# Order edges on VectorE in the transition from cross-attention to the FFN of a hybrid decoder layer

## The chip, the cores and the metric

The kernel runs on one core of a Trainium2 chip. The metric is the device time of one execution in microseconds (us). The median of three runs of the kernel before is 1662.94 us (1659.94 to 1664.27).

## What is computed

One decoder layer over 1024 rows of width 1024, in float32: a sparse and a differential attention with one input projection, a cross-attention to 256 memory rows, and a gated FFN with a causal convolution of width 3. The change touches the seam between the last two:

```python
h = h + cross_attention(rmsnorm(h, g_xattn), rmsnorm(mem, g_mem), w_xq, w_xk, w_xv, w_xo, g_xq, g_xk)
h = h + conv_glu(rmsnorm(h, g_ffn), w_ffn_in, conv_w, conv_b, w_ffn_out)

def rmsnorm(x, g):
    return x * rsqrt(mean(x * x, axis=-1) + EPS) * g

def conv_glu(hn, w_ffn_in, conv_w, conv_b, w_ffn_out):
    a, gate = split(hn @ w_ffn_in, 2)                 # 1024 x 2816 each
    conv = conv_b + sum(a_pad[:, j:j + S] * conv_w[j] for j in range(3))
    return (gelu(conv) * gate) @ w_ffn_out
```

## The kernel before, in words

**Arithmetic.** Every float32 product is made of three matmuls on high and low parts (mm3, lines 307 to 310). So each operand is split first: ScalarE or GpSimd casts the high part, VectorE or GpSimd subtracts it for the low part (L201, L203 and L204 for weights, L1330 and L1333 for activations). The FFN's input product is a block scheme with seven products instead of eight (P1, P2, P3, T1, T2, T3, T4 below), on sums and differences of quarter blocks. The activations' blocks are B11, B21, B22 and the sums T1 to T4; the weights' sums are made anew for each f.

**Rows and weights.** The 1024 rows are eight row blocks t of 128 rows. The FFN's 2816 columns are 22 groups f of 128. The weights of one f come as two raw tiles (a and g) and go through five jobs in this order: A (two pages from a), S (three VectorE additions, L225 to L227: `ws`, g and a change in place), B (two pages and one more subtraction, L233), C (two pages), D (one page). A page is a high and a low part, ready for TensorE; there are 12 page buffers. There are two raw buffers in the transition and a third from f = 1 on, and the next load (L188, on SyncE's queue, which issues nothing else there) starts when the last reader of a raw buffer is done. `W.pump(n)` (line 260) traces up to n jobs if pages are free by its own count; `W.get` traces jobs until the wanted page exists.

**The transition (lines 1603 to 1615).** For t = 0 to 7: `xo_unit(1, t)` (line 1287) makes the second half of the cross-attention's output product of row block t, adds it into h2[t] on VectorE (L1298), and in the middle of its matmuls calls `f_tr(t - 2)`; it ends with `W.pump(1)`. Then `f_norm(t)` (line 1303) normalizes: the squares are summed on ScalarE (L1133), `rstd1` (line 129) makes the reciprocal root with two VectorE instructions (L133, L134: the second is the first guess) and ten dependent ScalarE instructions on one column (L137), and two VectorE instructions scale the row block (L1313). `f_tr(t)` (line 1365) transposes the row block on TensorE (L1379). For t below 4 it splits the halves into B11 and B21. For t from 4 on it makes block sums: VectorE adds high and low part of B11 (L1344), GpSimd those of B21 (L1344), VectorE the low part of B22 (L1333), a piece of T1 (L1392) and of T2 (L1394), GpSimd pieces of T3 and T4 (L1396, L1398). Both PSUM buffers named trp are in use while one row block is transposed.

**After the loop** follow: P1 of f = 0 (on B11), `f_tr(6)`, P2 (on B21) with its addition (L1453), `f_tr(7)`, P3 (on B22, with a page of job C), the split of T1 to T3 (1024 columns each, L1358 and L1359) and T4, and then T2, T1, T3, T4 of f = 0. For f from 1 to 21 `ffn_in` (line 1447) makes seven products, seven VectorE additions that empty PSUM (L1453), a convolution (ScalarE L1494, VectorE L1495 and L1496), a gelu (L1497) and a product on GpSimd (L1502). GpSimd also makes sums for the FFN's output product (L1549). The second raw pool and the work tiles of f = 1 take over the memory of the transition's work tiles.

**What sets the order.** Each engine runs its instructions in a fixed order that is made when the kernel is built. The builder walks a simulated timeline and, for each engine, takes the first ready instruction in the order of tracing. Inside `manual_schedule` TensorE's own instructions keep the order of tracing among themselves. For the other engines nothing but readiness and that order decides, so later work that is ready passes earlier work that waits.

By trace order in the kernel before, the jobs of f = 0 are traced here: A in `xo_unit(1, 0)`, S in `xo_unit(1, 1)`, B in `xo_unit(1, 2)`, C in `xo_unit(1, 7)`, D with T2.

Of the kernel before, what the change touches and what calls it, by code (L numbers as in the profile page):

```python
# [11 lines left out]
BF = mybir.dt.bfloat16  # L12
I32 = mybir.dt.int32
AF = mybir.ActivationFunctionType
OP = mybir.AluOpType
# [5 lines left out]
D = 1024  # L21
NT = 8
# [22 lines left out]
def hybrid_layer(ctx, tc, I, out):  # L45
    nc = tc.nc
    pe, act, dve, pool, sp = nc.tensor, nc.scalar, nc.vector, nc.gpsimd, nc.sync
# [81 lines left out]
    def rstd1(r, ss, scale):  # L129

        w = small("rst", (P, 3, 8), 4)
        m, y, t, u = (w[:, 0, j:j + 1] for j in range(4))
        dve.tensor_scalar(m, ss, scale, EPS, op0=OP.mult, op1=OP.add)  # L133
        dve.tensor_scalar(y.bitcast(I32), m.bitcast(I32), -0.5, 1597463007.0, op0=OP.mult, op1=OP.add)  # L134

        def mul(o, x, f, bias=0.0):
            act.activation(o, x, AF.Copy, bias=bias, scale=f)  # L137
        mul(t, y, y)
        mul(t, t, m)
        mul(t, t, -3.0 / 16, 9.0 / 16)  # L140
        mul(y, y, t)
        mul(t, y, y)
        mul(t, t, m)
        mul(u, t, 64.0 / 9, -10.0 / 3)
        mul(t, t, u)
        mul(t, t, 64.0 / 9, 5.0)
        mul(r, t, y)


    NRAW, NWP = 2, 12  # L150
# [125 lines left out]
    W = Weights()  # L276
# [673 lines left out]
    for s in range(-4, NB):  # L950
        h, i = b_units[max(s, 0)]
        m = s % NT
# [178 lines left out]
    def norm_rows(src, jk, ssq, r):  # L1131

        act.activation(jk, src, AF.Square, accum_out=ssq)  # L1133
        rstd1(r, ssq, 1.0 / D)

    hx, hx_h = {}, {}

# [146 lines left out]
    h2 = []  # L1284
    hf, hst = {}, {}

    def xo_unit(c, t, mid=None):
        pages = W.get(("xo", c), 8)
        half, u = divmod(t, 4)
        p = accp()  # L1290
        for k in range(KT):
            oh, ol = ox[k // 4, (k % 4) // 2, half]
            s = slice(u * P, (u + 1) * P)
            if k == 4 and mid:
                mid()
            mm3(p, oh[:, k % 2, s], ol[:, k % 2, s], pages[k][:, 0, :], pages[k][:, 1, :], k == 0, k == KT - 1)
        hs = h2[t][:, c * 512:(c + 1) * 512]
        dve.tensor_tensor(hs, p, hs, op=OP.add)  # L1298
        if t == NT - 1:
            W.free(8)  # L1300
        W.pump(1)

    def f_norm(t):
        rs = slice(t * P, (t + 1) * P)
        act.dma_start(h2_d[rs, :], h2[t])
        st = small("st", (P, 12), 6)
        ws = [w2([P, 512], F32, "hn") for _ in range(1 if t >= 4 else 2)]
        norm_rows(h2[t], ws[0].bitcast(BF), st[:, 0:1], st[:, 1:2])
        hn = []
        for g in range(2):  # L1310
            hg = h2[t][:, g * 512:(g + 1) * 512]
            w = hg if t >= 4 else ws[g]
            dve.scalar_tensor_tensor(w, hg, st[:, 1:2], gff[g], op0=OP.mult, op1=OP.mult)  # L1313
            hn.append(w)
        hst[t] = hn

# [46 lines left out]
    def f_tr(t):  # L1365
        half, u = divmod(t, 4)
        if t == 0:
            xb_new("B11")
            xb_new("B21")
        if t == 4:  # L1370
            xb_new("B22")
            for n in ("T1", "T2", "T3"):
                tf[n] = [page([P, 2, 512], F32, n) for _ in range(2)]
        hn = hst.pop(t)
        ps_ = []
        for g in range(2):
            p = trp()
            for j in range(4):
                pe.transpose(p[:, j * P:(j + 1) * P], hn[g][:, j * P:(j + 1) * P], ident)  # L1379
            ps_.append(p)  # L1380
            if half == 0:
                xb_put(("B11", "B21")[g], u, p, "a", "d")
        if half == 0:
            return
        x11, x21 = xb_sum("B11", u, dve), xb_sum("B21", u, pool)
        ss = slice(u * P, (u + 1) * P)
        t1, t2, t3 = ([tf[n][v][:, :, ss] for v in range(2)] for n in ("T1", "T2", "T3"))
        t4s.append(x21)
        vs = [slice(0, 256), slice(256, 512)]
        xb_put("B22", u, ps_[1], "a", "d")  # L1390
        for v in range(2):
            dve.tensor_tensor(t1[v], two(ps_[0][:, vs[v]]), two(x11[:, vs[v]]), op=OP.subtract)  # L1392
        for v in range(2):
            dve.tensor_tensor(t2[v], two(ps_[1][:, vs[v]]), t1[v], op=OP.subtract)  # L1394
        for v in range(2):
            pool.tensor_tensor(t3[v], t2[v], two(x11[:, vs[v]]), op=OP.subtract)  # L1396
        for v in range(2):
            pool.tensor_tensor(two(x21[:, vs[v]]), two(x21[:, vs[v]]), t2[v], op=OP.subtract)  # L1398
# [28 lines left out]
    gff = []  # L1427
# [3 lines left out]
    for t in range(4, NT):  # L1431
        xo_unit(0, t)
# [169 lines left out]

    with tc.manual_schedule(engines={mybir.EngineType.PE}):
        for t in range(NT):
            xo_unit(1, t, (lambda: f_tr(t - 2)) if t >= 2 else None)
            f_norm(t)
        first = ffn_in(0)
        next(first)
        f_tr(6)
        next(first)  # L1610
        f_tr(7)
        next(first)
        for n in ("T1", "T2", "T3", "T4"):
            xb_finish(n)
        for _ in first:
            pass
# [119 lines left out]
```

## Time and profile before

| | us |
|---|---|
| median of three runs | 1662.94 |
| the profiled execution, whole | 1662.24 |
| its span, first to last instruction | 1660.4 |
| TensorE busy in the span | 1572.2 (95%) |
| VectorE busy | 1208.5 (73%) |
| ScalarE busy | 803.7 (48%) |
| GpSimd busy | 639.1 (38%) |
| mean granted TensorE clock | 0.978 |

The transition lies near 940 to 1045 us of the span, the FFN's input products run on to about 1447 us, the output products to the end. Times in the rows are counted from the span's start. A share of busy time is a mean over all stages of the kernel.

### The profile page before, as it was taken

The page shows a single profiled execution, that of the slowest core. Times are in us where ns is not written, and L with a number is a line of the kernel's source. Part 1 is how long each engine was busy: PE and PEld are TensorE (multiplying, and loading weights), DVE is VectorE, ACT ScalarE, POOL GpSimd, SP SyncE. Part 2 cuts the span into 40 slices and gives each one's busy share as a digit, 9 for nine tenths or more (in the row PEclk, how much of TensorE's full clock was granted, in tenths as well). Part 3 has the DMA queues.
Part 4 walks back from the last instruction along what each step waited for, and adds up shares of the span by engine and source line. Part 5 has one row for each costly group of instructions (what it writes and reads, how often), then busy time and mean ns, then how long its engine had stood idle before and what let it go on. Part 6 is the DMA issues. An engine that isn't in the chain of part 4 may idle for free.

```text
span 1660.4 us, 22257 instructions
## 1 busy us (share of the span) xinstructions
PE 1572.2 (95%) x7596; PEld 1271.6 (77%) x7596; DVE 1208.5 (73%) x2356; ACT 803.7 (48%) x1696; POOL 639.1 (38%) x888
## 2 busy tenths in 40 slices
PE   8899898888789999999999997999999999999999
PEld 7788675666668888878777775888887777888887
DVE  5738888878868875345544379989999999855554
ACT  6556665677877446428442265433333333343432
POOL 2735776223351131031101023666666666551111
PEclk9999998989989999999999998999999999999999
DMA  8320236221210122152203121455555555799812
GB/s 284 102 83 32 91 128 216 77 78 47 64 64 27 52 96 70 67 181 102 89 1 114 40 97 57 167 191 179 176 180 180 183 184 179 262 361 366 305 52 76
DMA packets 112162, 220.06 MB, mean 133 GB/s; under 512 B 18480, under 2 KB 38448, under 8 KB 112048
## 3 DMA queue, kind: packets, MB, share of 16 engines
q1 hardware_dynamic: 91072, 148.37, 26.7%
q0 software_dynamic: 18384, 61.36, 10.4%
q10 hardware_dynamic: 2592, 8.91, 1.4%
q8 instruction: 60, 0.98, 0.2%
q14 instruction: 54, 0.44, 0.1%
HBM read 160.92 MB, written 57.67 MB: 132 GB/s over the span
## 4 chain that ended last, share of the span: by engine, by line
PE 68%; DVE 16%; DMA 6%; ACT 4%; issue 3%; POOL 2%; SPq 0%; ACTq 0%; POOLq 0%; DVEq 0%
PE acc L308 11%; PE acc L310 10%; PE acc L309 10%; PE big L309 4%; PE big L308 4%; PE big L310 4%; PE trp L308 3%; PE trp L309 3%; PE trp L310 3%; PE acc L1036 3%; PE acc L885 2%; DVE jk L565 2%; DVE wp L204 2%; PE trp L691 2%; PE big L1275 2%
## 5 line engine op out<-in xcount | busy, mean ns | idle before, releaser
L204 DVE TENSOR_TENSOR wp<-raw,wp 128x512 fp32r<-128x512 f32 (+1 forms) x184 | 186.1, 1021 | 28.1 <-ACT wp L201 17.8
L201 ACT CAST wp<-raw 128x512 fp32r<-128x512 f32 (+1 forms) x184 | 108.3, 614 | 178.0 <-DVE raw L227 121.0
L1600 DVE TENSOR_TENSOR wp<-fo,wp 128x1024 fp32r<-128x1024 f32 x77 | 102.4, 1344 | 76.8 <-ACT wp L1599 69.2
L1549 POOL TENSOR_TENSOR fs<-fs,fs 128x512 f32<-128x512 f32 x88 | 128.5, 1460 | 64.3 <-DMA fs<-u_d 49.1
L1599 ACT CAST wp<-fo 128x1024 fp32r<-128x1024 f32 x77 | 79.8, 1049 | 107.9 <-PE trp L310 43.1
L308 PE MATMUL acc<-wp,xh 128*128 128x512 f32 (+1 forms) x272 | 109.6, 405 | 3.0 <-ACT X L646 3.0
L309 PE MATMUL acc<-wp,xh 128*128 128x512 f32 (+1 forms) x272 | 109.0, 401 | 0.0
L310 PE MATMUL acc<-wp,xl 128*128 128x512 f32 (+1 forms) x272 | 108.7, 400 | 0.0
L553 ACT ACTIVATE mb<-sc,cand 128x384 bf16<-128x384 f32 (+1 forms) x96 | 75.4, 786 | 35.9 <-DVE cand L557 30.5
L203 POOL TENSOR_SCALAR wp<-raw 128x512 fp32r<-128x512 f32 (+1 forms) x36 | 24.5, 685 | 176.8 <-DVE rst L110 63.6
L682 ACT COPY pt<-trp 128x512 f32<-128x512 f32 (+3 forms) x144 | 66.1, 475 | 40.6 <-PE trp L691 40.3
L1036 PEld LDWEIGHTS acc<-va_t,pt 128*128 128x128 f32 x576 | 75.2, 196 | 9.1 <-ACT pt L682 7.2
L1036 PE MATMUL acc<-va_t,pt 128*128 128x65 f32 x576 | 77.8, 274 | 3.7 <-ACT pt L682 3.6
L1646 POOL TENSOR_TENSOR hr<-hr,r 128x512 f32<-128x512 f32 x16 | 26.8, 1691 | 114.6 <-DVE r L1662 62.9
L1018 DVE CUSTOM_DVE_ANT_0 ea<-big,mb,ra 128x384 f32<-128x384 f32 (+5 forms) x48 | 45.4, 945 | 28.7 <-PE trp L691 25.1
L308 PEld LDWEIGHTS acc<-wp,xh 128*128 128x128 f32 x272 | 52.4, 193 | 15.0 <-ACT X L646 3.7
L1497 ACT ACTIVATE fc<-fc 128x1024 f32<-128x1024 f32 x22 | 23.4, 1062 | 82.9 <-DVE fc L1496 82.8
L204 POOL TENSOR_TENSOR wp<-raw,wp 128x512 fp32r<-128x512 f32 x36 | 47.2, 1325 | 40.5 <-ACT wp L201 40.1
L1019 ACT ACTIVATE ea<-ea,sta 128x128 f32<-128x128 f32 (+7 forms) x64 | 49.6, 776 | 25.7 <-DVE sta L1018 23.5
L1494 ACT ACTIVATE fc<-fa,cw 128x1024 f32<-128x1024 f32 x22 | 27.4, 1244 | 71.4 <-DVE fa L1453 71.4
L309 PEld LDWEIGHTS acc<-wp,xh 128*128 128x128 f32 x272 | 52.3, 192 | 11.3 <-issue 0.2
L310 PEld LDWEIGHTS acc<-wp,xl 128*128 128x128 f32 x272 | 52.1, 192 | 11.4
(422 smaller groups left out, 5113.7 us busy)
## 6 DMA issues: line engine op xcount, KB each, us to landing
raw<-in_w_ffn_in_dram SPq DMA_DIRECT2D x44, 512.0 KB, 4.1
fs<-in_w_ffn_out_dram POOLq DMA_DIRECT2D x44, 256.0 KB, 3.5
ws_d<-fs POOLq DMA_DIRECT2D x44, 256.0 KB, 2.3
fs<-u_d POOLq DMA_DIRECT2D x44, 256.0 KB, 3.8
us_d<-fs POOLq DMA_DIRECT2D x44, 256.0 KB, 3.2
fo<-us_d SPq DMA_DIRECT2D x44, 256.0 KB, 5.4
fo<-ws_d SPq DMA_DIRECT2D x44, 256.0 KB, 5.4
u_d<-fg POOLq DMA_DIRECT2D x21, 512.0 KB, 3.7
```

The lines of the kernel that those rows point to most:

```text
L201: act.copy(pg[:, 0, :n], src)
L204: (dve if el == "d" else pool).tensor_tensor(pg[:, 1, :n], src, pg[:, 0, :n].bitcast(F32), op=OP.subtract)
L308: pe.matmul(o, lhsT=lh, rhs=rh, start=start, stop=False)
L309: pe.matmul(o, lhsT=lh, rhs=rl, start=False, stop=False)
L310: pe.matmul(o, lhsT=ll, rhs=rh, start=False, stop=stop)
L553: act.activation(mb[i], sc[i], AF.Sign, bias=cf[:, j:j + 1], scale=-1.0, accum_out=cnt[:, j:j + 1])
L682: act.copy(dst, src)
L1019: last["act"] = act.activation(e[:, :n], e[:, :n], AF.Exp, bias=st[:, 0, h:h + 1], scale=-1.0)
L1036: pe.matmul(acc[:, hh * 65:hh * 65 + 65], lhsT=pt, rhs=va_t[:, kt, :], start=kt == 0, stop=kt == i)
L1549: pool.tensor_tensor(o, p, q, op=op)
L1599: act.copy(hi, raw)
L1600: dve.tensor_tensor(lo, raw, hi.bitcast(F32), op=OP.subtract)
```

## The change

`rstd1` and `norm_rows` return the VectorE instruction of the first guess (L134), and `f_norm` returns that one and its last scaling instruction (L1313): `guess` and `scaled`. `tc.issue_after(x)` lets every VectorE instruction traced inside its block be ordered behind x on VectorE. It is an order only, not a wait for x to finish, and it binds no other engine.

- The unit `xo_unit(1, 7)`, with `f_tr(5)` in it, comes behind the guess of row block 6.
- `f_tr(6)` comes behind the guess of row block 7.
- P2's addition, and the first weights' jobs S and B, come behind the scaling of row block 7. P1 carries no VectorE instruction.
- In the second pass (c = 1) `xo_unit` doesn't pump while the next job is an S. So after A of f = 0 nothing is pumped; S and B of f = 0 are traced by a new `W.pump(2)` between `f_tr(6)` and P2, and C by P3's `W.get`.

No instruction is added or taken away.

```diff
-        dve.tensor_scalar(y.bitcast(I32), m.bitcast(I32), -0.5, 1597463007.0, op0=OP.mult, op1=OP.add)
+        guess = dve.tensor_scalar(y.bitcast(I32), m.bitcast(I32), -0.5, 1597463007.0, op0=OP.mult, op1=OP.add)
...
+        return guess
...
-        rstd1(r, ssq, 1.0 / D)
+        return rstd1(r, ssq, 1.0 / D)
...
         if t == NT - 1:
             W.free(8)
-        W.pump(1)
+        if c == 0 or W.jobs[W.nsplit][4] != "S":
+            W.pump(1)
...
-        norm_rows(h2[t], ws[0].bitcast(BF), st[:, 0:1], st[:, 1:2])
+        guess = norm_rows(h2[t], ws[0].bitcast(BF), st[:, 0:1], st[:, 1:2])
...
-            dve.scalar_tensor_tensor(w, hg, st[:, 1:2], gff[g], op0=OP.mult, op1=OP.mult)
+            scaled = dve.scalar_tensor_tensor(w, hg, st[:, 1:2], gff[g], op0=OP.mult, op1=OP.mult)
...
+        return guess.ins, scaled.ins
...
         for t in range(NT):
-            xo_unit(1, t, (lambda: f_tr(t - 2)) if t >= 2 else None)
-            f_norm(t)
+            with tc.issue_after(guess) if t == NT - 1 else ExitStack():
+                xo_unit(1, t, (lambda: f_tr(t - 2)) if t >= 2 else None)
+            guess, scaled = f_norm(t)
         first = ffn_in(0)
-        next(first)
-        f_tr(6)
-        next(first)
+        with tc.issue_after(scaled):
+            next(first)
+        with tc.issue_after(guess):
+            f_tr(6)
+        with tc.issue_after(scaled):
+            W.pump(2)
+            next(first)
         f_tr(7)
         next(first)
```

## Rows read from the trace of the kernel before

**Rows 1.** The page: busy tenths in 40 slices, then one line of DMA issues.

```profile
PE   8899898888789999999999997999999999999999
DVE  5738888878868875345544379989999999855554
...
raw<-in_w_ffn_in_dram SPq DMA_DIRECT2D x44, 512.0 KB, 4.1
```

**Rows 2.** Windows: length, busy us (count) PE, PEld, DVE, ACT, POOL; PEclk; DMA, GB/s.

```profile
940.00:950.00 10.00, 10.00 (x46) 8.20 (x45) 7.92 (x12) 2.58 (x5) 0.14 (x1) 1.00 0.32 105
...
995.00:1000.00 5.00, 0.00 (x0) 0.00 (x0) 5.00 (x9) 3.37 (x10) 5.00 (x6) 0.89 0.60 207
1000.00:1005.00 5.00, 1.27 (x6) 1.30 (x7) 5.00 (x7) 2.58 (x14) 2.42 (x3) 0.50 0.00 0
...
1035.00:1040.00 5.00, 5.00 (x23) 3.98 (x22) 4.25 (x6) 1.79 (x3) 0.00 (x0) 1.00 0.82 276
1040.00:1045.00 5.00, 5.00 (x23) 4.03 (x22) 3.13 (x6) 3.17 (x4) 3.88 (x4) 1.00 0.54 176
...
1280.00:1300.00 20.00, 18.57 (x79) 14.34 (x79) 18.86 (x20) 6.50 (x10) 14.34 (x16) 1.00 0.59 197
```

**Rows 3.** Timeline of TensorE in the transition: start, length, line; in brackets idle before.

```profile
1003.73 1.94 PE L1379 MATMUL trp<-ident,h 128*128 128x128 f32 x8 [9.10 <-issue]
...
1022.52 0.50 PE L309 MATMUL big<-T,wp 128*128 128x512 f32 x1 [1.16 <-DVE T L1359]
```

**Rows 4.** Timeline of VectorE, 988 to 1006 us.

```profile
988.21 1.21 DVE L204 TENSOR_TENSOR wp<-raw,wp 128x512 fp32r<-128x512 f32 x1
...
993.04 0.14 DVE L134 TENSOR_SCALAR rst<-rst 128x1 int32<-128x1 int32 x1
...
995.86 2.59 DVE L1344 TENSOR_TENSOR xf<-B,B 128x256 f32<-128x256 f32 x3
998.37 1.21 DVE L225 TENSOR_TENSOR ws<-raw 128x512 f32<-128x512 f32 x1
999.50 0.14 DVE L134 TENSOR_SCALAR rst<-rst 128x1 int32<-128x1 int32 x1
...
1002.89 1.40 DVE L1313 SCALAR_TENSOR_TENSOR h<-h,st,gff 128x512 f32<-128x512 f32 x2
...
1004.82 1.40 DVE L1313 SCALAR_TENSOR_TENSOR h<-h,st,gff 128x512 f32<-128x512 f32 x2
```

**Rows 5.** Timeline of ScalarE: the column chain of row block 0.

```profile
951.27 2.63 ACT L137 ACTIVATE rst<-rst 128x1 f32<-128x1 f32 x9 [0.41 <-DVE rst L134]
...
954.14 0.29 ACT L137 ACTIVATE st<-rst 128x1 f32<-128x1 f32 x1 [0.24 <-ACT rst L137]
```

**Rows 6.** Timeline of VectorE: first and last instruction of S and B, f = 0.

```profile
945.10 0.69 DVE L225 TENSOR_TENSOR ws<-raw 128x512 f32<-128x512 f32 x1 [0.22 <-DMA raw<-in_w_ffn_in_dram]
...
949.21 0.68 DVE L204 TENSOR_TENSOR wp<-ws,wp 128x512 fp32r<-128x512 f32 x1
```

**Rows 7.** Timeline of VectorE: first convolution step of f = 2 and of f = 19.

```profile
1070.17 1.46 DVE L1495 SCALAR_TENSOR_TENSOR fc<-fa,cw,fc 128x1023 f32<-128x1023 f32 x1 [0.78 <-ACT fc L1494]
...
1418.04 1.46 DVE L1495 SCALAR_TENSOR_TENSOR fc<-fa,cw,fc 128x1023 f32<-128x1023 f32 x1 [0.78 <-ACT fc L1494]
```

**Rows 8.** Timeline of TensorE: T4 of f = 2, of f = 3, last idle time.

```profile
1064.73 0.39 PE L308 MATMUL big<-T,wp 128*128 128x512 f32 x1
...
1084.33 0.39 PE L308 MATMUL acc<-T,wp 128*128 128x512 f32 x1
...
1410.47 0.50 PE L308 MATMUL acc<-T,wp 128*128 128x512 f32 x1 [0.94 <-DVE fa L1453]
```

**Rows 9.** Waits of TensorE, 1024 us to the end: total, times, longest.

```profile
PE acc L308 <- DVE fa L1453: 2.4, 2, 1.4
PE big L308 <- DVE fa L1453: 1.0, 2, 0.6
PE trp L308 <- DVE fa L1453: 1.0, 1, 1.0
```

## The prediction

> **What bounds the kernel now.** I read the page's slices first [rows 1]. TensorE is at nine tenths nearly everywhere; slice 25 of 40, 996 to 1038 us, falls to seven tenths: the transition. VectorE is at eight or nine tenths from there to slice 35. So at the seam two engines are candidates, and the change moves work from one place on VectorE to another.
>
> The windows show how the seam fails [rows 2]. From 995 to 1000 us TensorE does nothing and VectorE has no free moment. TensorE's timeline gives the size: 9.10 us idle ahead of the transposes of row block 6, and 1.16 us ahead of T2 [rows 3]. The granted clock is 0.89 from 995 to 1000 us and 0.50, the lower level of 1.2 GHz, from 1000 to 1005 us [rows 2]; the stretch before it is the idle one. VectorE's timeline says why [rows 4]: the guess of row block 6 starts at 993.04, its scaling only at 1002.89. ScalarE needs 951.27 to 954.43, 3.2 us, for the column chain between them when nothing disturbs it [rows 5]. In between VectorE makes block sums (three L1344, 2.59 us) and the first sum of the weights of f = 1 (L225, 1.21 us) ahead of row block 7's guess at 999.50, and ScalarE's fixed order mixes the two chains. That is what the edges forbid.
>
> Next, whether this lost time reaches the end. TensorE passes T4 of f = 2 at 1064.73 and T4 of f = 3 at 1084.33: 19.60 us for one f [rows 8]. VectorE's first convolution step starts at 1070.17 for f = 2 and at 1418.04 for f = 19: 347.87 us for 17 steps, 20.46 us each [rows 7]. So VectorE is slower by 0.86 us per f, 14.6 us over the 17. TensorE waited only 2.4 + 1.0 + 1.0 = 4.4 us in all that time, always for the VectorE additions that empty PSUM [rows 9], last at 1410.47 [rows 8]. The other 10 us went into lead: TensorE ran further and further ahead until PSUM was full. My reading: from the transition to 1410 us VectorE sets the pace, and TensorE has some 10 us to give away. A microsecond that TensorE wins at the seam is waited out later; one that VectorE loses there arrives at the end.
>
> **The change, part by part.**
>
> *The edges on the guesses.* They take L204 (1.21 us), L1344 and others from between the scaling of row block 5 and the guess of row block 6 [rows 4]. That scaling ends where L204 starts, at 988.21, and the squares are ready by then, so the guess falls from 993.04 to about 988.6. With the chain (3.2 us, and about 0.5 for casts in between) the scaling of row block 6 can start near 992.5. Row block 7 depends on the last output product, which doesn't move; I put its guess at 995.2 (before 999.50), its chain's end at 998.9, and `scaled` done at about 1000.4 (before 1004.82 + 1.40 = 1006.2). So the transposes of row block 6 start near 995 instead of 1003.73, and most of the 9.10 us goes.
>
> *What is late next.* S, B and C of f = 0 now all stand behind `scaled`, and P3 needs a page of C. From 1000.4 VectorE has S (3), B (3), C (2) and P2's addition, nine instructions at 0.68 us [rows 6], 6.1 us, and among them the pieces of `f_tr(7)`, some 2 us. So P3 starts near 1008 to 1009. In the kernel before it followed the 1003.73 transposes, P2 and `f_tr(7)`, which I put at 1012.5 by their lengths at the low clock. TensorE is then some 4 us earlier, no longer 9: a second idle stretch takes the place of the first. Behind these instructions on VectorE queue T1 to T3; TensorE's T2 waits for them.
>
> *S and B moved.* Before, they ran from 945.10 to 949.89, with one output addition of 0.6 us between, so 4.2 us [rows 6], where VectorE had 2.1 us of 10 free [rows 2] and no one waited. Now they lie in a stretch where VectorE has no idle time until 1035. The cover is gone: +4.2 us on VectorE. Bounds: 6 x 0.68 = 4.1, and 6 x 1.21 = 7.3 if all meet GpSimd as L225 and L204 did in the seam [rows 4].
>
> *What runs beside GpSimd.* The same instruction has 0.68 us when GpSimd is idle [rows 6] and 1.21 us beside its block sums [rows 4]. The jobs A and S of f = 1 now come after the block sums; S, B, C of f = 0 take their place. Bounds: none, and nine instructions cheaper by 0.53, -4.8 us. I take -1.5, near none, because one set replaces another.
>
> *New idle time on VectorE.* Two chains of 3.2 us, 6.3 us in all, in which VectorE may not run ahead. It is still allowed the pieces of row block 5, the output addition and one scaling under the first, and the pieces of row block 6 under the second, about as much. Bounds 0 and 3; I take 1.
>
> *The idle time of before.* VectorE was idle 0.75 us in 1035 to 1040 and 1.87 us in 1040 to 1045 [rows 2], where work of f = 1 waited for the memory and the end of f = 0. f = 0 now ends earlier, but the weights of f = 1 come later: the load of its first raw tile waits for the last page of C, and has 4.1 us to landing [rows 1]. SyncE's queue has nothing else behind it; VectorE's own queue does, if a sum of f = 1 stands ahead. Bounds 0 and -2.6; I take -1.2.
>
> The casts of S, B and C on ScalarE and GpSimd's block sums carry no edge; they follow their inputs, and they are no new work. Nothing else is added.
>
> *Sum for VectorE.* 4.2 - 1.5 + 1.0 - 1.2 = +2.5 us at the point where the loop over f has its steady order, and with that order, which comes from buffers and pages and not from the seam, +2.5 us at the end. The profiled execution took 1662.24 us, 0.70 below the median. 1662.24 + 2.5 = 1664.7 us. The ends of the terms give 4.1 - 4.8 + 0 - 2.6 = -3.3 and 7.3 + 0 + 3 + 0 = +10.3.
>
> A rule bears on the choice of engine. In 1280 to 1300 us weight loads fill 14.34 of 20 us and VectorE 18.86 [rows 2]. The Trainium skill (Perfetto Trace Analysis, Identifying the Most-Contended Engine) judges TensorE by its weight loads and not by matmul busy time, and improves the engine with the highest occupancy; by that rule VectorE is the engine here, and the trace agrees. The same page (Optimization Strategies) says to treat whatever blocks an idle matmul engine, since its idle time is the loss; that is the rival below.
>
> **The rivals.**
>
> *Faster: TensorE sets the pace.* If VectorE's 20.46 us per f are only a shadow of late inputs and its order behind the seam gets looser, TensorE's gain at P3 stays: 4 us, with the 1.16 us before T2 5 us: 1662.24 - 5 = 1657 us; with the whole 9.10 us, 1653. For it speaks that TensorE is busy over nine tenths and VectorE has about a tenth of idle time in the loop. Against it: all 4.4 us of TensorE's waits are for VectorE, and TensorE's lead grew by 10 us without any wait of VectorE for TensorE in the rows I read. Perfetto Trace Analysis (Optimization Strategies) of the Trainium skill would give this side; the rows bear it out at the seam and not behind it.
>
> *Slower: the first weights come too late.* S, B and C are a chain across VectorE and ScalarE, and the raw buffers of f = 0 come free only after C and D; so the weights of f = 1 start some 8 to 10 us later than before. The place is the stretch from P3 to f = 1's T2. If VectorE has to stand idle there for the loads, by more than the 2.6 us that it stood idle before, or if S and B meet GpSimd at 1.21 us, its delay is 7.3 - 1.5 + 1 + 0 = +6.8 and more: 1669 us. The point from which it decides is 5 us of VectorE delay at the convolution of f = 2.
>
> *The edges do nothing.* If the builder's order already had the guesses first, only the move of S and B would be left, +4 us. The rows speak against it: L1344 and L225 stand right ahead of row block 7's guess [rows 4]. It lies inside the forecast's band.
>
> **How the numbers follow.** Within 0.3% is 5.0 us of 1662.94, about what a measurement of this kernel can tell from no change: 1657.9 to 1667.9. Forecast 1664.7, no measurable change: 0.50. TensorE's gain stays, faster: 0.26. The late weights, slower: 0.24. Both sides leave a tail out of the range: 1656 below (the first rival's 1657 with 1 us for the spread of runs) and 1670.5 above (the second's 1669 and 1.5). The likeliest case's own range is 1659 to 1668.
>
> **What would show it.** Right: the guess of row block 6 starts near 989 and that of row block 7 near 995; the 9.10 us gap ahead of the transposes of row block 6 is under 2 us; a new idle stretch of 5 us or more stands ahead of P3; TensorE's T4 of f = 2 is earlier by some 4 us while L1495 of f = 2 is later by 0 to 5 us and the step per f stays near 20.46; TensorE's waits for L1453 after 1024 us grow from 4.4 to 10 us or more. Wrong: the step per f changes, which would make the pace of VectorE no constant of the loop; or L1495 of f = 2 comes earlier than 1070.17 by more than 3 us, which would mean that my sum for VectorE misses a saving; or TensorE's waits don't grow though it starts earlier.

## The result, and the profile after

The changed kernel takes 1679.95 us (median of 4 runs, 1674.93 to 1684.11) beside 1661.76 us for the kernel before on the same chip: 1.0106 times as long, with a 95% interval of 1.0082 to 1.0130, some 18 us. The profiled execution of the changed kernel took 1684.11 us with a span of 1682.3. That is the slowest of its four runs, so the delays read from its trace add up to more than 18 us. Its output addition of row block 2 starts 0.64 us later than before (960.10 against 959.46); "net" below means that such an offset is taken off. This point lies behind the old place of S and B: ahead of it, at the last output addition of the first half, the offset is 1.23 us (942.70 against 941.47). So the kernels that hold S and B back win 0.6 us there, and their net delays, counted from row block 2, are 0.6 us larger than counted from ahead of the change.

VectorE's timeline in the transition (start, length, engine, line; in brackets the idle time before), to be read against [rows 4]. Line numbers are higher by up to 3 in the changed kernel, and in some experiments by more: L134 is the guess, L1315 the scaling, L226 the first of S, L205 a low part, L1347 a block sum.

```profile
989.00 0.15 DVE L134 TENSOR_SCALAR rst<-rst 128x1 int32<-128x1 int32 x1
...
996.15 0.15 DVE L134 TENSOR_SCALAR rst<-rst 128x1 int32<-128x1 int32 x1
996.22 3.33 DVE L1347 TENSOR_TENSOR xf<-B,B 128x256 f32<-128x256 f32 x4
...
1001.99 2.23 DVE L1315 SCALAR_TENSOR_TENSOR h<-h,st,gff 128x512 f32<-128x512 f32 x2
1004.15 1.21 DVE L226 TENSOR_TENSOR ws<-raw 128x512 f32<-128x512 f32 x1
...
1014.10 2.94 DVE L205 TENSOR_TENSOR wp<-raw,wp 128x512 fp32r<-128x512 f32 x3
```

Both guesses come earlier, by 4.0 and 3.4 us, as the edges want. The last scaling ends at 1004.2 and not at 1000.4. From there to the last low part of C, at 1017.0, it is 12.9 us, where I had counted 6.1 and 2.

TensorE's timeline, to be read against [rows 3]:

```profile
996.19 0.63 PE L1382 MATMUL trp<-ident,h 128*128 128x128 f32 x4 [0.52 <-DVE rst L133]
...
1003.19 1.09 PE L1382 MATMUL trp<-ident,h 128*128 128x128 f32 x4 [3.56 <-issue]
...
1010.71 0.79 PE L309 MATMUL big<-B,wp 128*128 128x512 f32 x1 [5.26 <-ACT wp L202]
...
1016.49 0.79 PE L311 MATMUL big<-B,wp 128*128 128x512 f32 x1 [4.56 <-DVE wp L205]
```

The stall of 9.10 us ahead of row block 6 is 0.52 us now, inside its transposes. In its place stand 3.56 us ahead of row block 7, 5.26 us ahead of P3 and 4.56 us inside it, for the high and the low parts of f = 0's weights: with the 0.52 they are 13.9 us. The windows (columns as in [rows 2]) show what follows for the clock:

```profile
1000.00:1005.00 5.00, 1.72 (x7) 1.38 (x8) 4.56 (x8) 1.06 (x4) 3.32 (x5) 0.72 0.00 0
1005.00:1010.00 5.00, 0.45 (x3) 0.05 (x1) 5.00 (x10) 4.05 (x7) 0.94 (x1) 0.50 0.00 0
...
1015.00:1020.00 5.00, 3.51 (x8) 2.81 (x9) 5.00 (x6) 2.16 (x5) 0.89 (x1) 0.50 0.47 135
1020.00:1025.00 5.00, 5.00 (x18) 3.90 (x17) 5.00 (x11) 2.37 (x6) 0.00 (x0) 0.73 0.20 79
```

The granted clock is 0.50, the lower level of 1.2 GHz, from 1005 to 1020 us, and at that level for part of the time on either side. It fell behind TensorE's first idle stretch, which begins at 999.6, and was back at 1.00 by 1025 us, TensorE being busy without a gap from 1016.49 on.

Farther on, TensorE's T4 of f = 2 and of f = 3, then VectorE's first convolution step of f = 2 and of f = 19, against [rows 7] and [rows 8]:

```profile
1069.31 0.40 PE L309 MATMUL big<-T,wp 128*128 128x512 f32 x1
...
1088.91 0.40 PE L309 MATMUL acc<-T,wp 128*128 128x512 f32 x1
```

```profile
1081.01 2.81 DVE L1498 SCALAR_TENSOR_TENSOR fc<-fa,cw,fc 128x1023 f32<-128x1023 f32 x1
...
1434.95 1.47 DVE L1498 SCALAR_TENSOR_TENSOR fc<-fa,cw,fc 128x1023 f32<-128x1023 f32 x1 [0.78 <-ACT fc L1497]
```

T4 comes 4.6 us later, not 4 us earlier. The convolution of f = 2 is 10.8 us later, that of f = 19 16.9: 353.94 us for 17 steps, 20.82 each, where it was 20.46. TensorE's waits from 1024 us to the end (total, times, longest), against the 4.4 us of [rows 9]:

```profile
PE big L309 <- DVE fa L1456: 4.5, 5, 1.5
PE acc L309 <- DVE fa L1456: 3.9, 4, 1.7
PE acc L309 <- DVE fg L1456: 3.2, 1, 3.2
PE trp L309 <- DVE fa L1456: 3.2, 3, 1.7
```

With three small groups for v (2.6 us) they are 17.4 us. So the loss in this trace has three places: about 10 us at the seam, 6 in the loop, 4 in the last f. The loop and the last f are not touched by the change.

### The profile page after: what moved, and what is told of

Same layout as the page of the kernel before. It is cut to its first block, busy times and chain, and to the rows that moved or that the text cites. A ratio compares the mean times of both kernels' runs of the same rounds, so it can differ in the third digit from the quotient of the medians.

```text
span 1682.3 us, 22262 instructions
## 1 busy us (share of the span) xinstructions
PE 1575.4 (94%) x7596; PEld 1272.1 (76%) x7596; DVE 1201.0 (71%) x2356; ACT 803.7 (48%) x1696; POOL 640.5 (38%) x888
## 3 DMA queue, kind: packets, MB, share of 16 engines
q0 software_dynamic: 18384, 61.36, 10.4%
## 4 chain that ended last, share of the span: by engine, by line
PE 56%; DVE 21%; DMA 10%; ACT 5%; issue 4%; POOL 3%; SPq 0%; ACTq 0%; DVEq 0%; POOLq 0%
PE acc L309 9%; PE acc L311 9%; PE acc L310 9%; DVE wp L205 4%; PE big L311 3%; PE big L309 3%; PE big L310 3%; PE acc L1037 3%; DMA raw<-in_w_ffn_in_dram 3%; DMA fs<-u_d 2%; PE acc L886 2%; PE trp L692 2%; POOL fs L1552 2%; DVE jk L566 2%; PE big L1276 2%
## 5 line engine op out<-in xcount | busy, mean ns | idle before, releaser
L205 DVE TENSOR_TENSOR wp<-raw,wp 128x512 fp32r<-128x512 f32 (+1 forms) x184 | 180.9, 996 | 26.6 <-ACT wp L202 15.9
L205 POOL TENSOR_TENSOR wp<-raw,wp 128x512 fp32r<-128x512 f32 x36 | 47.7, 1338 | 40.1 <-ACT wp L202 34.6
```

The lines of the kernel that those rows point to most:

```text
L205: (dve if el == "d" else pool).tensor_tensor(pg[:, 1, :n], src, pg[:, 0, :n].bitcast(F32), op=OP.subtract)
```

## Experiments

The table puts all runs side by side. "Late" is the net delay of VectorE's first convolution step against the kernel before, worked out from the profiled execution: start of that step less start of the output addition of row block 2, and the same of before taken off. For the two kernels without sums (e9, e10) e10 is compared with e9. "Load first" says whether, on GpSimd's queue from f = 6 on, a load of output-weight rows stands ahead of the product of an even f; what that is comes below. Times in us with a difference are medians; the ratios can differ from them by up to 2 us (e14: 6.9 us by medians, 8.5 by the ratio).

| run | time / time before (95%) | late f = 3 | f = 19 | f = 21 | load first |
|---|---|---|---|---|---|
| changed kernel | 1.0106 (1.0082 to 1.0130) | +10.2 | +16.3 | +19.8 | yes |
| e1 edges only | 1.0144 (1.0121 to 1.0168) | +6.4 | +12.1 | +19.5 | yes |
| e2 move only | 1.0014 (0.9995 to 1.0033) | -0.2 | +0.1 | +0.5 | no |
| e3 VectorE more | 1.0124 (1.0097 to 1.0150) | +8.5 | +9.4 | +14.6 | yes |
| e4 TensorE more | 1.0108 (1.0086 to 1.0129) | +4.8 | +8.5 | +14.1 | yes |
| e5 late sums | 1.0116 (1.0092 to 1.0140) | +11.8 | +16.0 | +19.6 | yes |
| e6 edge on unit 7 | 1.0072 (1.0048 to 1.0096) | +2.6 | +9.6 | +12.6 | yes |
| e7 edge on f_tr(6) | 1.0003 (0.9987 to 1.0019) | +1.5 | +1.4 | +1.7 | no |
| e8 edges on blocks | 1.0001 (0.9986 to 1.0016) | -0.2 | +0.3 | +0.5 | no |
| e10 without sums, against e9 | 1655.77 / 1654.00 us | +3.0 | +3.0 | +3.0 | none |
| e11 half the order | 1.0120 (1.0092 to 1.0148) | +10.5 | +17.5 | +18.2 | no |
| e12 before, load first | 1.0083 (1.0051 to 1.0116) | 0.0 | +8.9 | +14.0 | yes |
| e13 changed, order of before | 1.0063 (1.0039 to 1.0087) | +10.4 | +9.7 | +11.1 | no |
| e14 e4, order of before | 1.0051 (1.0035 to 1.0067) | +5.3 | +2.0 | +4.8 | no |
| e15 e3, order of before | 1.0049 (1.0029 to 1.0069) | +8.6 | +8.4 | +10.3 | no |
| e16 product earlier | 1.0017 (1.0003 to 1.0031) | +0.1 | 0.0 | +3.5 | no |
| e17 e1, order of before | 1.0020 (1.0006 to 1.0034) | +6.3 | +3.4 | +4.4 | no |
| e18 e5, order of before | 1.0051 (1.0033 to 1.0070) | +10.7 | +7.1 | +8.9 | no |

### The two halves of the change, and the two engines (e1 to e4)

e1_edges_only keeps the edges and lets S and B of f = 0 run early, as before:

```diff
-        if c == 0 or W.jobs[W.nsplit][4] != "S":
-            W.pump(1)
+        W.pump(1)
...
-            W.pump(2)
```

> The three order edges without the move: S and B of f = 0 stay where they were, near 945 us. Theory (the moved weight jobs cost the time, because VectorE sets the pace from the seam on): 1660 to 1668 us, and VectorE's first convolution step of f = 2 no more than 3 us later than before. Rival (the edges themselves cost, because VectorE may not run ahead during the norm chains): 1672 us or more.

Measured 1682.30 beside 1659.12 us: the rival's number. The edges without the held sums cost no less than the whole change.

e2_move_only takes the edges away and keeps the move:

```diff
-        with tc.issue_after(scaled):
-            W.pump(2)
-            next(first)
+        W.pump(2)
+        next(first)
```

> S and B of f = 0 held back until behind f_tr(6), without any order edge. Theory (the move costs): 1668 to 1680 us. Rival (the edges cost): 1660 to 1666 us.

Measured 1661.13 us, no change: without an edge S of f = 0 still starts at 943.7, because the order on VectorE is the builder's and not that of the text.

e3_dve_twice and e4_pe_twice are the kernel before with more work on one engine: 14 low parts of f = 1 and 2 twice on VectorE, or T2 and T1 of f = 2 twice on TensorE (24 matmuls, 5.6 us).

```diff
+            for _ in range(2 if twice else 1):
+                (dve if el == "d" else pool).tensor_tensor(pg[:, 1, :n], src, pg[:, 0, :n].bitcast(F32), op=OP.subtract)
...
+        for k in list(range(4)) * (2 if nprod[0] in (16, 18) else 1):
```

> The kernel before, in which VectorE makes the low part of the fourteen weight pages of f = 1 and f = 2 twice: the same values, 14 instructions more of 0.68 to 1.1 us, 9.5 to 15 us of VectorE. Theory (VectorE sets the pace up to 1410 us): all of it arrives at the end, 1671 to 1678 us. Rival (TensorE sets the pace, VectorE has room): 1660 to 1665 us.

> The kernel before, in which TensorE makes two products of f = 2 twice into the same PSUM bank: 24 matmuls more, 5.6 us of TensorE. Theory (TensorE has some 10 us to give away): 1661 to 1664 us, and TensorE's waits for the additions that empty PSUM shrink from 4.4 us. Rival (TensorE sets the pace): 1667 to 1669 us.

Measured 1678.73 and 1675.94 us. TensorE was to have 10 us to give away; 5.6 us of it cost 16.8. And a delay of VectorE of 8.5 us cost 19.6. Whatever is delayed at the seam seems to grow by about 10 us on the way to the end. That was the open point from here on.

### Which part of the change (e5 to e8)

One part each on the kernel before: S and B held and put behind the last scaling without norm edges (e5); the edge on the unit of row block 7 (e6), on `f_tr(6)` (e7), on the first two blocks of f = 0 (e8). The lines added in each:

```diff
+        with tc.issue_after(scaled):
+            W.pump(2)
...
+            with tc.issue_after(guess) if t == NT - 1 else ExitStack():
...
+        with tc.issue_after(guess):
...
+        with tc.issue_after(scaled):
+            next(first)
```

> The kernel before with one part of the change: the block sums of the first weights (S of f=0, and B behind them) are held and put behind the last norm scaling, with none of the edges on the row blocks' norm steps. Theory (what costs is VectorE's list growing between the seam and the convolution of f=2; the held sums are the part of it that is 4 to 6 us of VectorE): the convolutions of f=2 and f=3 come 3 to 6 us later than before and the time is 1664 to 1672. Rival (the norm edges cost it all, the held sums are worth nothing or a little as against the edges alone): within 3 us of before, about 1660.

> The kernel before with one edge alone: the output unit of the last row block (and the transposes of block 5 inside it) put behind the inverse root's guess of block 6. Theory (the costly edges are those that hold FFN work, the two behind the last scaling): within 3 us of before, about 1660. Rival (pulling guess 6 ahead of the block sums of f=1 and of block 5's work is what fills the list): +8 us or more, 1670 or above.

> The kernel before with one edge alone: the transposes and block sums of row block 6 put behind the guess of block 7. Theory: the guess of block 7 no longer waits behind the block sums of 6; convolution of f=2 within 3 us of before; time about 1660. Rival (block 6's sums, put later, stand in the way of block 7's and of the first weights): convolution of f=2 5 us or more later, 1668 or above.

> The kernel before with the two edges on the first two products of f=0 alone (both behind the scaling of block 7): what they issue on VectorE and for the weights comes after the last norm step. Theory (these edges push the weights' work of f=0 and f=1 together behind the seam, where GpSimd's first sums start, so VectorE's operations there take longer): convolution of f=2 at 1076 or later and 1670 to 1682. Rival (they cost little without the other edges): under 1665.

Measured 1681.43, 1674.98, 1662.69 and 1661.57 us. The parts don't add up: two cost nothing, one 13 us and one 20, the edges together 23, the whole 18. e6 has its rival's time but not its reason: it is 2.6 us late at f = 3 and 12.6 at f = 21. That the edges with FFN work behind them are the costly ones is refuted by e8; e5 is worse than either side expected.

### Without GpSimd's sums (e9, e10)

What is left in the loop and at its end is GpSimd. There it makes the gated product of each f (`fg`, L1502 before and L1505 after), stores it, and in `fo_sums` loads blocks of output weights and of stored products, adds them and stores the sums. e9 and e10 leave these sums out, with their loads and stores; the last stage loads plain blocks in their place.

```diff
-            owed_sums.extend(fo_sums("w", f // 2))
+            pass
...
-            owed_sums.extend(fo_sums("u", f // 2 - 1))
+            pass
```

> The kernel before without the sums of output weights and of activations that GpSimd makes in the loop (their loads and stores are gone too; the last stage loads plain blocks in their place, as many of the same size). Both theories: shorter than before, since VectorE no longer shares with GpSimd in the loop; it is the base of the next run.

> The changed kernel without the same sums and transfers. With the sums, the change cost 18 us: 10 by the convolution of f=2, 6 over f=3 to f=19, 4 from f=20 to f=21. Theory (GpSimd's sums and their round trips turn a delay of 10 us into 18): against the run without sums of the kernel before it is 6 to 11 us longer and the loop's step is the same within 0.1 us. Rival (the loop's slower step and its end come from TensorE, VectorE and the weights' loads alone): 15 us or more longer, with a step 0.3 us or more longer, as with the sums.

Measured 1654.00 and 1655.77 us, too near to each other to be told apart (0.9953, 0.9937 to 0.9968, and 0.9964, 0.9952 to 0.9976, of before). Neither side of e10's expectation has that time, 6 us more or 15 us more; the theory's equal step came true. One window of each, 1100 to 1400 us, first of e9, then of e10:

```profile
1100.00:1400.00 300.00, 300.00 (x1288) 241.70 (x1287) 230.15 (x306) 108.44 (x154) 44.54 (x30) 1.00 0.23 78
```

```profile
1100.00:1400.00 300.00, 300.00 (x1288) 241.70 (x1287) 229.44 (x306) 108.41 (x154) 44.54 (x30) 1.00 0.23 78
```

TensorE is busy for 300 of 300 us, the step is 19.60 in both, and VectorE has 70 us free. The changed seam is 6.8 us late at f = 1, 5.4 at f = 2 and 3.0 from f = 3 to the end. So here TensorE sets the pace, VectorE takes its delay back, and what is left is TensorE's own loss at the seam: a loss, no gain, in the very case in which my faster rival wanted 5 to 9 us won. With the sums and their transfers, 16 us more are lost.

### GpSimd's queue (e11 to e13)

The traces of GpSimd around the product of f = 10, before:

```profile
1241.05 0.55 POOL L1545 DMA_DIRECT2D fs<-u_d  x1
1241.62 2.40 POOL L1502 TENSOR_TENSOR fg<-fc,fg 128x1024 f32<-128x1024 f32 x1
1243.96 0.58 POOL L1545 DMA_DIRECT2D fs<-in_w_ffn_out_dram  x1
```

and after:

```profile
1251.43 0.55 POOL L1548 DMA_DIRECT2D fs<-u_d  x1
1251.97 0.55 POOL L1548 DMA_DIRECT2D fs<-in_w_ffn_out_dram  x1
1252.54 2.41 POOL L1505 TENSOR_TENSOR fg<-fc,fg 128x1024 f32<-128x1024 f32 x1
```

The builder put the queue in another order. With G the product, U its store, y a load of output-weight rows, x a load of activations, s a sum and w its store, the stretch from one odd product to the next is:

```
before, e2, e7, e8:              s U w xxx sw sw sw x   G y s U w yy sw sw sw y  G
changed, e1, e3 to e6, and e12:  s U w xxx sw sw sw x y G   s U w yy sw sw sw y  G
e11:                             s U w xxx sw sw sw x   G y U s w yy sw sw sw y  G
e13 to e15, e17, e18:            s U w xxx sw sw sw x   G y s U w yy sw sw sw y  G
e16:                             U s w xxx sw sw sw   G x y U s w yy sw sw sw y  G
```

The builder gave six kernels the load first, and they are 13 us or more slower than before; the three to which it gave the other order aren't slower. Only f = 6 on is compared here; the queues differ at f = 2 to 5, too. The load changes places at f = 6, 8, ... 20 (eight times; the expectation says nine).

e12_before_load_first gives the kernel before that order by an edge, with the product traced later; the other engines' order is unchanged in its trace. e11_after_product_first takes it from the changed kernel by an edge on the load:

```diff
+            with tc.issue_after(prods[2 * m].ins) if m >= 3 else ExitStack():
+                x["11"] = ld(0, 0)
```

e13_after_queue_of_before adds a second edge, so that the product's store stands behind the last sum, too: before's order. Of the other queues only SyncE's differs from the changed kernel's, in the place of a few loads at the end of the loop.

```diff
+            with tc.issue_after(last_sum[0].ins):
+                stores.pop(f - 1)()
```

> The changed kernel with one more edge: from f=6 on, the first load of output-weight rows for GpSimd's next block sums is issued behind the gated product of the even f on GpSimd's queue, as it stands in the kernel before; in the changed kernel that load stands ahead of the product (nine times). The other engines' order stays that of the changed kernel. Theory (the loop's slower step and its late end come from that place in GpSimd's queue, where the product now stands behind a load that waits for a buffer): the step falls from 20.9 to about 20.5, the last step from 22.8 to about 19.5, and the time from 1680 to 1667 to 1672; the 10 us by the convolution of f=2 stay. Rival (a seam that is 10 us late slows the loop, whatever GpSimd's order): 1678 to 1682, step 20.8 or more.

> The kernel before with GpSimd's queue alone changed the other way: from f=6 on, the first load of output-weight rows for the next block sums stands ahead of the gated product of the even f, as in the changed kernel. The seam and the other engines' order are as before. Theory (that place in GpSimd's queue costs by itself): step 20.8 to 20.9, last step 22 or more, time 1668 to 1674. Rival (GpSimd's order is a consequence that costs nothing): within 3 us of before.

> The changed kernel with GpSimd's queue from f=6 on in the order of the kernel before: product, first load of output-weight rows, the last sum, then the product's store (two edges; TensorE's, VectorE's and ScalarE's order is that of the changed kernel). Theory (GpSimd's order is 13 of the 18 us, the seam the rest): step 20.5 to 20.6, PE's waits for additions under 8 us, time 1664 to 1670. Rival (the late seam by itself slows the loop and the end): step 20.8 or more, 1676 or above.

Measured 1681.54, 1674.22 and 1670.92 us; e12 is 0.2 and e13 0.9 above what was expected, and e13 has 9.6 us of TensorE's waits for additions, where under 8 were expected. e12 settles that the order costs by itself: nothing at the seam, 0.0 us at f = 3, 14.0 at f = 21. e13 settles that in the changed kernel it costs some 9 of the 18 us (each of the two ratios is known to 4 us): the step from f = 3 to f = 19 is 20.48, where it was 20.52 before and 20.90 in the changed kernel, and the delay of f = 3, 10.4 us, arrives as 11.1. e11 missed: one edge gives a third order (U ahead of s), and that is as slow as the second, with a step of 20.96. So it isn't the product's wait alone.

What the order does to VectorE is seen in its groups over the same 16 steps, f = 3 to f = 19 (busy us, mean ns, then idle before). Kernel before:

```profile
L204 DVE TENSOR_TENSOR wp<-raw,wp 128x512 fp32r<-128x512 f32 x96 | 112.5, 1172 | 4.4 <-ACT wp L201 4.4
L1496 DVE SCALAR_TENSOR_TENSOR fc<-fa,cw,fc 128x1022 f32<-128x1022 f32 x16 | 35.6, 2226 | 0.0
...
L225 DVE TENSOR_TENSOR ws<-raw 128x512 f32<-128x512 f32 x16 | 14.9, 932 | 12.6 <-DMA raw<-in_w_ffn_in_dram 12.6
```

e12, before with the load first:

```profile
L204 DVE TENSOR_TENSOR wp<-raw,wp 128x512 fp32r<-128x512 f32 x96 | 100.2, 1044 | 4.4 <-ACT wp L201 4.4
L1510 DVE SCALAR_TENSOR_TENSOR fc<-fa,cw,fc 128x1022 f32<-128x1022 f32 x16 | 41.7, 2609 | 0.0
...
L225 DVE TENSOR_TENSOR ws<-raw 128x512 f32<-128x512 f32 x16 | 15.4, 962 | 28.6 <-DMA raw<-in_w_ffn_in_dram 28.6
```

The changed kernel:

```profile
L205 DVE TENSOR_TENSOR wp<-raw,wp 128x512 fp32r<-128x512 f32 x96 | 102.8, 1071 | 4.4 <-ACT wp L202 4.4
L1499 DVE SCALAR_TENSOR_TENSOR fc<-fa,cw,fc 128x1022 f32<-128x1022 f32 x16 | 40.3, 2518 | 0.0
...
L226 DVE TENSOR_TENSOR ws<-raw 128x512 f32<-128x512 f32 x16 | 14.8, 925 | 27.1 <-DMA raw<-in_w_ffn_in_dram 27.1
```

e13, the changed kernel with before's order:

```profile
L205 DVE TENSOR_TENSOR wp<-raw,wp 128x512 fp32r<-128x512 f32 x96 | 113.7, 1184 | 5.4 <-ACT wp L202 5.4
L1508 DVE SCALAR_TENSOR_TENSOR fc<-fa,cw,fc 128x1022 f32<-128x1022 f32 x16 | 34.1, 2131 | 0.0
...
L226 DVE TENSOR_TENSOR ws<-raw 128x512 f32<-128x512 f32 x16 | 20.0, 1253 | 8.5 <-DMA raw<-in_w_ffn_in_dram 8.4
```

The two orders leave the same print in both kernels. With the load first VectorE is less busy in the low parts (100 to 103 us for 113) but waits 27 to 29 us for the raw tile of S instead of 8 to 13, and the second convolution step is 5 to 8 us dearer. One reading: an instruction that GpSimd slows down while VectorE is under way to a load costs nothing, since the wait behind it shrinks; the same collision in the convolution isn't given back. That fits these rows and e11 (S waits 6.5 us, but VectorE is busy for 313.6 us, 12.8 more than before).

The traces hold a rival that no run tests: with the load first, the raw tile itself lands later. The raw tiles' loads from f = 3 to f = 19, from issue to landing, in the kernel before, in e12, in the changed kernel and in e13:

```profile
DMA to landing us min/median/max: 3.1/4.2/5.0
DMA to landing us min/median/max: 3.2/4.3/7.3
DMA to landing us min/median/max: 3.1/4.4/7.3
DMA to landing us min/median/max: 3.2/4.0/5.0
```

Loads of over 6 us are found in six kernels alone, all with the load first (29 in all), and each has two loads of GpSimd issued in the 1.5 us ahead of it: without the product between them, these two now stand together. Not every such pair makes one: e16 has pairs, behind the product, and no load over 5.5 us. In the other kernels no raw tile takes more than 5.8 us. e3 has the load first but no raw load over 5.4 us, and it loses only 1.0 us from f = 3 to f = 19. So the longer waits of S are at least in part late loads. How much of the loop's loss is that, and how much collisions, is not shown; e11, without such loads, is slow for another reason.

The end is the other place. GpSimd and ScalarE in the changed kernel, at the product of f = 20:

```profile
1464.40 0.55 POOL L1548 DMA_DIRECT2D fs<-u_d  x1 [1.24 <-DMA us_d<-fs]
1466.55 0.55 POOL L1548 DMA_DIRECT2D fs<-in_w_ffn_out_dram  x1 [1.59 <-DMA us_d<-fs]
1467.12 2.40 POOL L1505 TENSOR_TENSOR fg<-fc,fg 128x1024 f32<-128x1024 f32 x1
```

```profile
1469.55 1.24 ACT L1497 ACTIVATE fc<-fa,cw 128x1024 f32<-128x1024 f32 x1 [7.23 <-POOL fg L1505]
```

The product stands behind two loads that wait for stores (1.24 and 1.59 us), and the convolution of f = 21 stands 7.23 us for the buffer that the product frees. Before, the product started at 1444.92, right behind a sum, and ScalarE waited for VectorE only.

### The delays once more, with the order kept (e14 to e18)

e14, e15, e17 and e18 are e4, e3, e1 and e5 with the two edges of e13.

> The kernel with two products of f=2 made twice on TensorE (5.6 us more there; 16 us longer than before) with GpSimd's queue from f=6 on in the order of the kernel before. Theory (most of the 16 us was GpSimd's order): 1662 to 1667, so that TensorE's 5.6 us cost no more than themselves. Rival (TensorE's delay is passed on and grows): 1672 or above.

> The kernel with 14 low-part subtractions made twice on VectorE for f=1 and f=2 (9.5 us more there or above; 19.6 us longer than before) with GpSimd's queue from f=6 on in the order of the kernel before. Theory (VectorE's 10 us are passed on as they are, the rest was GpSimd's order): 1668 to 1674. Rival (growth by the late seam itself): 1677 or above; and if VectorE's delay were taken up by TensorE's lead, 1663 or less.

> The changed kernel's edges on the norm steps without the held block sums (alone: 20 us longer than before), with GpSimd's queue from f=6 on in the order of the kernel before. Theory (the edges themselves are cheap: in the trace of the edges alone the convolution of f=2 came some 4 us late): 1664 to 1668. Rival (the edges are the seam's 9 us): 1669 or above.

> The held block sums of the first weights without the norm edges (alone: 20 us longer than before), with GpSimd's queue from f=6 on in the order of the kernel before. Theory (the late sums, which VectorE makes in the list between the seam and the convolution of f=2, are the seam's 9 us): 1668 to 1673. Rival (they are hidden): 1665 or less.

Measured 1668.78, 1668.21, 1663.59 and 1669.07 us, so +6.9, +6.4, +3.0 and +8.4 us. The growth is gone. The late sums alone cost about what the whole change costs with this order (9.1 us); the edges alone cost 3 us (e17 is 0.4 us under its expected range). e15 came out at the low edge of what was expected, and e14 1.8 us above it. Between f = 3 and f = 19 some of the delay is taken back (3.3 us in e14, 2.9 in e17, 3.6 in e18, 0.2 in e15); 1 to 3 us are lost again from f = 19 to f = 21, where these kernels' order isn't quite before's (before, the product of f = 20 stands two instructions farther ahead). So VectorE's delay in e15 is passed on whole through the loop (8.6 us, then 8.4). Of TensorE's 5.6 us in e14 VectorE has 5.3 at f = 3, 2.0 at f = 19 and 4.8 at f = 21: there was a lead, some 3 us and not 10, and nothing of it is seen in the time.

e16_before_product_earlier asks whether the kernel before can gain: one more load behind the product.

```diff
+                with tc.issue_after(prods[2 * m + 2].ins) if m < 10 else ExitStack():
+                    x["12"] = ld(1, 0)
```

> The kernel before with GpSimd's product of every even f put one load further ahead (the load for the last of the sums of activations, too, stands behind the product), one edge; the seam is untouched. If what costs in the changed kernel is a product that stands behind loads that wait for a buffer, this is the other direction: 1655 to 1661. If the order of before is only a lucky one, any change of it costs: 1665 or above.

Measured 1664.70 us, +2.9: neither. The loop is as before, and 3.5 us are lost from f = 19 to f = 21. No version that does all the work beat the kernel before.

## Why the prediction was wrong

It said no change, 1664.7 us, in a range to 1670.5; the time was 1680. Two steps failed, each worth about half.

**"That order, which comes from buffers and pages and not from the seam".** This is the step that carried +2.5 us unchanged to the end, and it was never tested against GpSimd. VectorE's order did stay the same from the convolution of f = 3 to that of f = 20, as its timelines show, and ScalarE's, too; GpSimd's did not, since the builder lays out the queues of the whole program anew. e12 prices that order at 13 us in the kernel before, e13 at 9 in the changed kernel. Its sign that I had named, a step per f that changes, is what appeared (20.46 to 20.82).

**The sum for VectorE.** It said +2.5 us at the convolution of f = 2; the net delay is 10.2, 7.0 of it busy time and 3.2 idle. Its terms, by the groups of VectorE from 988 us to that step, first before, then after (busy us, mean ns):

```profile
L204 DVE TENSOR_TENSOR wp<-raw,wp 128x512 fp32r<-128x512 f32 x24 | 20.4, 855 | 0.8 <-ACT wp L201 0.8
...
L204 DVE TENSOR_TENSOR wp<-ws,wp 128x512 fp32r<-128x512 f32 x4 | 2.7, 678 | 0.0
```

```profile
L205 DVE TENSOR_TENSOR wp<-raw,wp 128x512 fp32r<-128x512 f32 x25 | 25.4, 1040 | 0.0
...
L205 DVE TENSOR_TENSOR wp<-ws,wp 128x512 fp32r<-128x512 f32 x5 | 6.1, 1226 | 0.0
```

- S and B moved, +4.2: right as a count, VectorE has six instructions more in this stretch (122 for 116).
- Beside GpSimd, -1.5: wrong in sign. The other 2.8 us of busy time, 7.0 less 4.2, belong here. 28 low parts took 23.1 us, 30 take 31.5; S's sums, shorter than before, took part of that back. In e10 the same 30 take 25.2, and the delay at f = 2 is 5.4 us instead of 10.2. I had looked at GpSimd's sums of row blocks only; work pushed to the right meets the loop's sums, which begin behind 1040.
- The idle time, +1.0 and -1.2: VectorE's idle time in this stretch grew from 3.5 to 6.7 us, +3.2. Of the 6.7 us, 3.0 are waits for raw tiles and 2.6 for TensorE.

**TensorE 4 us earlier at P3, with 10 us of lead to give away.** P3 began at 1010.71 and stood another 4.56 us inside; T2 followed at 1020.92, where it was 1020.97. But by then the kernel before had also made P1 and T1 of f = 1 (24 matmuls, from 1012.80 and 1018.17 us), which now come later, and T4 of f = 2 is 4.6 us late. Behind row block 7's guess VectorE has row block 6's four block sums (3.33 us) and that block's low parts; ScalarE has the block's second cast in the middle of the chain and waits for VectorE there. The chain took 5.4 us for 3.2:

```profile
1000.58 0.37 ACT L1333 CAST B<-trp 128x256 fp32r<-128x256 f32 x1 [2.03 <-DVE B L1336]
```

And ahead of C's low parts stand two low parts of T1 to T3 (L1362, 1.21 us each) that I hadn't counted. The lead was an error of reading: TensorE's lead grows from f = 3 on, but up to there VectorE follows it closely, so that what TensorE loses at f = 1 to 3 VectorE loses, too (e14: 5.3 of 5.6 us at f = 3; the loop gave 3.3 of them back).

**The rivals.** The slower one named the right place and price. Its point of decision, 5 us of VectorE delay at the convolution of f = 2, was passed (10.2), and its 1669 us is near what the changed kernel takes once GpSimd's order is kept (1670.92; 6.8 us by its sum, 9.1 measured); e18 puts it on the late sums. It had no word on GpSimd's order either. It deserved the highest chance: the terms on which I set it aside (-1.5 and -1.2) were the two with the least support in rows. The faster one is refuted even with TensorE as the pace (e10). That the edges do nothing was true of two of them (e7, e8).

Right were: the early guesses; the stall ahead of row block 6 gone, and a new one of over 5 us at P3; TensorE's waits for additions above 10 us (17.4), but these by luck: they were to grow because TensorE came earlier, and it came later.

**On the rule of highest occupancy** that was weighed: VectorE is the fuller engine in the loop, and the trace agrees with that; but a delay of either engine at the seam lengthened the kernel (e14, e15), so occupancy didn't tell which one could be spared.

## What to carry to other kernels

When a builder lays out the queues, compare every engine's order before and after, those the change doesn't name first of all: here a load ahead of a product on GpSimd, 150 us and more behind the edit, cost as much as the edit itself. An effect that doesn't add up over the parts of a change, and grows far from it, points to such an order; fix it with edges before the parts are priced. And work that is moved out of a place where nobody waits is priced by the row of the place it goes to, with the engine that is busy there.

## What was not expected of the hardware

The low part of S's sum (128x512) has a mean of 0.68 us from 988 us to the convolution of f = 2 before and of 1.23 there after. From f = 3 to f = 19 the 96 low parts of raw tiles take 81.0 us in the kernel without GpSimd's sums and 112.5 with them, and the second convolution step 1275 ns against 2226. The additions that empty PSUM, with one operand in SBUF, keep 0.68 to 0.69 us in both. The Trainium skill (SBUF — State Buffer, Who interferes with whom) says that VectorE and GpSimd share a pair of ports under an exclusive lock, and that nothing else among the engines contends; the trace agrees for the two in so far as VectorE's instructions with both operands in SBUF are longer beside GpSimd's, and no run here shows the lock itself. What the runs add: the cost depends on which VectorE instructions meet GpSimd's, and more of them isn't always worse. From f = 3 to f = 19 VectorE is busy for 303.5 us in e13 and for 292.9 in e12, and yet e13's stretch is 9.5 us shorter (327.63 against 337.16); late raw tiles are part of that.

Without GpSimd's sums and their transfers the loop runs at TensorE's 19.60 us per f from f = 3 on, in both kernels: the 20.46 us of the kernel before are VectorE beside GpSimd and its transfers (no run separates the two), not VectorE's work by itself.
